# Two-layer encoder on one core: a gate half computed earlier, a turn moved to TensorE, and a bias table read backwards through GpSimd's queue

## The chip, the core and the metric

The kernel runs on one core of one Trainium2 chip. A core has five engines with a queue of instructions each: TensorE (PE in the profile, with the loads of its weights as PEld), VectorE (DVE), ScalarE (ACT), GpSimd (POOL) and SyncE (SP), which here only starts transfers. Each takes its own queue in order, and they wait for each other by semaphores. The metric is device microseconds of one execution of the whole program. Three runs of the kernel before took 883.23, 883.34 and 884.79 us, a median of 883.34 us.

## The reference

The input is one sequence of 256 tokens with 1024 channels in float32. Two layers follow each other, then a last normalisation. In short:

```
h = x
for layer in range(2):
    xn = rmsnorm(h) * norm1
    u, q, k, v, g_pool, g_attn = split(xn @ w_in)      # 1024 x 7680
    pool = centred means of u over 2/4/8/16 tokens, minus u, times w_pool
    attn = three groups of four heads, windows of 129 keys at stride 1, 4, 16,
           logits + bias(relative position), softmax over all three groups
    merged = sigmoid(g_pool) * (pool @ w_a) + sigmoid(g_attn) * (attn @ w_b)
    h += merged @ w_o
    xn = rmsnorm(h) * norm2
    a, g = split(xn @ w_up)                            # 1024 x 5632
    h += (gelu(conv3(a)) * g) @ w_down
out = rmsnorm(h) * norm_f
```

The bias depends only on the distance between query and key. The tokens are held by even and odd position, so that a tile of 128 queries against 128 keys needs 255 distances for each of five kinds of pair.

## The kernel before, in words

Every float32 product is made of three products of rounded parts: a value is split into a high part (`wh`, `xh`, written by ScalarE as a copy, line 179) and a low part (`wl`, the rest, by VectorE as a subtraction, line 180), and TensorE adds high times high, high times low and low times high. So each weight piece of 128 x 1024 numbers costs one ScalarE cast and one VectorE subtraction before TensorE may use it.

The class `Weights` orders this. All weights of the program stand in one list, in the order of their use. SyncE loads them, 1 MB at a time, into three buffers (`raw`); each load serves two pieces; a piece goes into one of five pairs of buffers (`wh`, `wl`). `get` hands out a piece and has the next three (`LOOK`) split ahead. A `raw` buffer is free when both of its pieces are split, a `wh`/`wl` pair when TensorE is through with it. Some pieces at the beginning of a sub-layer get buffers of their own (`slots`). The order on each engine is set by a scheduler that places the instructions by their estimated readiness; the order on one engine is then fixed.

A layer goes through these stages, each with TensorE as the engine that all feed:

- values, pooling inputs, queries and keys, by `proj` (16 products a piece, lines 490 and 492);
- the stage called gates here, by `by_rows` (line 594): products of 128 x 512, twelve for each piece. One of its halves is 512 of the 1024 output channels. The kernel before does the pool gate (`C_GP`, 8 pieces), then `w_a` (8 pieces), then for each half the attention gate (`C_GA`, 4 pieces) and `w_b` (2 pieces). `po2` holds the pooled part, `at2` the attention's, `pa` what the pool branch gives, `th` the merged rows of a half.
- in between, `step` puts in the attention of the first heads at numbered visits, one visit after each piece: scores, turning of the probabilities, their parts, and the weighting. `VISITS` has the numbers.
- `w_o`, by `residual_mm` (line 521): eight pieces, each against the merged rows turned into channels (`m2`, high part `mh`, low part `ml`). Pieces 0 to 3 are added into four accumulators as they come; pieces 4 to 7 are held, and the accumulators are finished one after another, so that the normalisation of the first tokens starts early.
- the MLP, in the same manner, its first four pieces from `w_up` in slots.

The merged rows have tokens on partitions, and `w_o` needs channels there. The kernel before turns the first half by one transposition in blocks of 32 on VectorE (line 1063) and 16 transfers between partitions (`cross`, line 609, `way<-way` in the profile) which SyncE starts during the second half; `merged_parts` splits what comes back (lines 1047 and 1048). The second half is turned on VectorE alone, by 32 transpositions of single blocks (`blocks`, line 617, tile `turned`), and split by lines 1077 and 1078.

The bias table is built once, in `build_bias`: TensorE sums the buckets, VectorE copies the rows to `fsb` (line 384), three transfers put them in one row in memory (`fd`, 20 KB), one transfer copies this row 128 times, each time one further (`sk`, 2.56 MB, line 393), and five transfers read from `sk` the table `bt` (line 398), with 128 keys for each of 128 queries. All nine are started by SyncE, between the weight loads. `bias_of` hands the part of `bt` to the addition at line 917.

Of the kernel before, what the change touches and what calls it, by code (L numbers as in the profile page):

```python
# [55 lines left out]
def _bias_table():  # L56

    t = np.zeros((33, NT, 256), np.float32)
    delta = np.arange(255) - 127
    for n, (e, dil) in enumerate(  # L60
        ((2 * delta, 1), (2 * delta + 1, 1), (2 * delta - 1, 1), (2 * delta, 4), (2 * delta, 16))
    ):
        valid = (e % dil == 0) & (np.abs(e) <= 64 * dil)
        b = _buckets(e)
        j = np.nonzero(valid)[0]
        t[b[j], n, j] = 1.0
        t[32, n, np.nonzero(~valid)[0]] = NEG
        t[32, n, 255] = NEG
    return t.reshape(33, NT * 256)


def _edge_table():
# [134 lines left out]
def encoder(ctx, tc, x, w_in, w_pool, pool_scale, w_a, w_b, w_o, norm1, norm2, w_up, conv_w,  # L207
# [166 lines left out]
    def build_bias(rr, ohr):  # L374

        fsb = big.tile([96, NT * 256], F32, tag="q1", name="fsb")
        for c0, groups in ((0, (0, 0)), (512, (0, 1)), (1024, (2,))):
            width = 256 * len(groups)
            ps = acc.tile([P, 512], F32, tag="acc", name="f_ps")
            nc.tensor.matmul(ps[:, :width], rr, ohr[:, c0 : c0 + width], start=True, stop=True)  # L380
            for j, g in enumerate(groups):
                cc = slice(j * 256, (j + 1) * 256)
                rows = slice(32 * g, 32 * g + HPG)
                nc.vector.tensor_copy(fsb[rows, c0 + j * 256 : c0 + (j + 1) * 256], ps[rows, cc])
            yield

        n = HPG * NT * 256
        fd = dram.tile([1, n], F32, name="fd")
        fv = fd[0].rearrange("(h e) -> h e", h=HPG)
        for g, cc in enumerate((slice(0, 768), slice(768, 1024), slice(1024, 1280))):  # L390
            nc.sync.dma_start(out=fv[:, cc], in_=fsb[32 * g : 32 * g + HPG, cc])
        sk = dram.tile([P, n + 1], F32, name="sk")
        nc.sync.dma_start(out=sk[:, 0:n], in_=fd[0].partition_broadcast(P))
        for blk, kind in enumerate((2, 0, 1, 3, 4)):
            src = bass.AP(
                sk.tensor, sk.offset + kind * 256 + 127, [[n, P], [NT * 256, HPG], [1, P]]
            )
            nc.sync.dma_start(out=bt[:, :, blk * P : (blk + 1) * P], in_=src)
# [386 lines left out]
    for l in range(DEPTH):  # L785
# [115 lines left out]
        def scores(hh):  # L901
            probs[hh] = sm.tile([P, 2, 512], F32, tag="s", name="probs")
            for t in range(2):
# [6 lines left out]
                for g in (1, 2):  # L910
# [4 lines left out]
                    )  # L915
                s = probs[hh][:, t]
                nc.vector.tensor_add(
                    out=s.rearrange("p (a b) -> p a b", a=2), in0=ps.rearrange("p (a b) -> p a b", a=2),
                    in1=bias_of(t, hh),
                )  # L920
                nm = sm.tile([P, 1], F32, tag="nm", name="nm")
                nc.vector.tensor_reduce(out=nm, in_=s, axis=AX.X, op=ALU.max, negate=True)
# [98 lines left out]
        for n, cc in enumerate(HALVES):  # L1021
# [5 lines left out]
        for cc in HALVES:  # L1027
            ps = by_rows(po2, 4, step)
# [5 lines left out]
        assert not any(visits) and not crossing  # L1034
        g2 = gain(norm2[l])


        m2 = big.tile([P, 2, KD, 2, P], F32R, tag="m2", name="m2")
        mh, ml = m2[:, 0], m2[:, 1]
        way = big.tile([P, 2, 4, 2, 4, 32], F32, tag="k1", name="way")  # L1040
        def merged_parts():
            yield from cross(way[:, 1], way[:, 0])
            yield
            for t in range(2):
                m = way[:, 1, :, t].rearrange("p i c r -> p c i r")
                hi, lo = (a[:, 0:4, t].rearrange("p c (i r) -> p c i r", i=4) for a in (mh, ml))
                nc.scalar.copy(out=hi, in_=m)  # L1047
                nc.vector.tensor_sub(out=lo, in0=m, in1=hi.bitcast(F32))

        for n, cc in enumerate(HALVES):  # L1050
            ps = by_rows(x2, 4, n and (lambda: next(first, None)))
            th = big.tile([P, 2, 512], F32, tag=("q0", "k0")[n], name="th")
            for t in range(2):
                nc.scalar.activation(th[:, t], ps[t], AF.Tanh, scale=0.5)
            ps = by_rows(at2, 2, n and (lambda: next(first, None)))
            for t in range(2):
                p = th[:, t]
                nc.vector.scalar_tensor_tensor(
                    out=p, in0=p, scalar=1.0, in1=ps[t], op0=ALU.add, op1=ALU.mult
                )  # L1060
                nc.vector.tensor_add(out=p, in0=p, in1=pa[:, t, cc])
            if n == 0:
                nc.vector.transpose(
                    out=way[:, 0].rearrange("p j t c r -> p (t c) j r"),
                    in_=th.rearrange("p t (c j r) -> p (t c) j r", c=4, j=4),
                )
                first = merged_parts()
            else:
                assert next(first, None) is None
                turned = big.tile([P, 4, 2, P], F32, tag="v0", name="turned")  # L1070
                for k in range(0, 4, 2):
                    run(blocks(
                        turned[:, k : k + 2].rearrange("p c t q -> p t c q"),
                        th[:, :, k * P : (k + 2) * P].rearrange("p t (c k) -> p t c k", c=2),
                    ))
                    hi, lo = (a[:, 4 + k : 6 + k] for a in (mh, ml))
                    nc.scalar.copy(out=hi, in_=turned[:, k : k + 2])
                    nc.vector.tensor_sub(out=lo, in0=turned[:, k : k + 2], in1=hi.bitcast(F32))

        x2 = two_parts("x", "x2")  # L1080
        norm = Norm(to_channels(x2, acc, g2))
# [137 lines left out]
```

## Time and profile before

| | |
|---|---|
| median of three runs | 883.34 us (883.23 to 884.79) |
| the profiled execution | 885.41 us, its span 883.6 us |
| TensorE busy | 864.5 us, 98% of the span |
| VectorE busy | 689.0 us, 78% |
| ScalarE busy | 496.1 us, 56% |
| transfers | 169.86 MB, 192 GB/s over the span |
| mean granted clock of TensorE | 0.994 |

A line of the timeline gives the start, the duration, the engine, the line of the kernel, the operation, the tile written and the tiles read, the shape and the count; in brackets stands the idle time of the engine before it, with what ended it. A start minus the start before it is the time that an instruction held its engine; the duration of a matmul reaches over the start of the next one, because they are pipelined. In the table of windows, PEclk is the clock that TensorE was granted, as a share of its full clock. SPq is SyncE's queue, where the bar is the time in which it issues a transfer, not the transfer.

### The profile page before, as it was taken

How to read it: one execution, taken by the hardware profiler on the slowest of the kernel's cores; microseconds unless marked ns; L12 is line 12 of the kernel's file. 1: busy time of each engine (PE TensorE's matmuls, PEld its weight loads, DVE VectorE, ACT ScalarE, POOL GpSimd, SP SyncE). 2: the span in 40 equal slices, each digit the busy share in tenths (PEclk: the TensorE clock that was granted, in tenths of full speed). 3: DMA queues.
4: the chain of work that ended last, by engine and by line, in shares of the span. 5: the costliest groups of instructions: out<-in, count | busy, mean ns of one | idle time of the engine just before them, and what ended most of it. 6: DMA issues, size and time to landing. Idle time of an engine off the chain costs nothing.

```text
span 883.6 us, 12221 instructions
## 1 busy us (share of the span) xinstructions
PE 864.5 (98%) x4538; PEld 740.3 (84%) x4538; DVE 689.0 (78%) x1148; ACT 496.1 (56%) x817; POOL 17.3 (2%) x45
## 2 busy tenths in 40 slices
PE   9999999999899999999999999999997999999997
PEld 7887988888778888888888899888885888888886
DVE  7996895756788998779755968785569799887884
ACT  7754654534436766667545555464443567666662
POOL 2000000000010000000000000000000100000000
PEclk9999999999999999999999999999999999999999
DMA  9677836565454475665726555547644556565541
GB/s 337 207 234 233 276 119 226 169 236 193 165 190 159 176 238 169 217 207 169 263 96 212 170 193 189 179 155 238 215 145 162 173 189 237 191 198 183 191 144 49
DMA packets 118408, 169.86 MB, mean 192 GB/s; under 512 B 4790, under 2 KB 84358, under 8 KB 118220
## 3 DMA queue, kind: packets, MB, share of 16 engines
q1 hardware_dynamic: 118332, 169.07, 57.0%
q8 instruction: 36, 0.59, 0.3%
q14 instruction: 24, 0.20, 0.1%
q10 hardware_dynamic: 16, 0.00, 0.0%
HBM read 162.74 MB, written 3.69 MB: 188 GB/s over the span
## 4 chain that ended last, share of the span: by engine, by line
PE 87%; DVE 5%; DMA 4%; SPq 2%; ACT 1%; issue 1%; POOL 0%; POOLq 0%; ACTq 0%
PE proj_ps L490 28%; PE rows_ps L587 15%; PE proj_ps L492 14%; PE v_ps L587 6%; PE res_ps L518 5%; PE res_ps L517 5%; PE res_ps L519 5%; PE v_ps L777 2%; DVE turned L617 2%; DMA sk<-fd 2%; PE v_ps L690 1%; DMA raw<-in_w_up_dram 1%; DVE wl L180 1%; SPq L609 1%; PE o_ps L968 1%; PE s_ps L911 1%
## 5 line engine op out<-in xcount | busy, mean ns | idle before, releaser
L180 DVE TENSOR_TENSOR wl<-raw,wh 128x1024 fp32r<-128x1024 f32 x274 | 332.6, 1221 | 114.1 <-ACT wh L179 111.7
L179 ACT CAST wh<-raw 128x1024 fp32r<-128x1024 f32 x274 | 285.4, 1048 | 172.7 <-PE proj_ps L490 63.2
L490 PE MATMUL proj_ps<-x,wh 128*128 128x512 f32 x1152 | 289.9, 394 | 1.8 <-ACT wh L179 1.8
L490 PEld LDWEIGHTS proj_ps<-x,wh 128*128 128x128 f32 x1152 | 209.0, 189 | 40.2 <-ACT wh L179 2.0
L492 PEld LDWEIGHTS proj_ps<-x,wl 128*128 128x128 f32 x1152 | 157.6, 191 | 11.4
L492 PE MATMUL proj_ps<-x,wl 128*128 128x256 f32 x1152 | 161.0, 282 | 0.0
L587 PE MATMUL rows_ps<-wh,x 128*128 128x512 f32 x256 | 80.9, 391 | 0.0
L517 PE MATMUL res_ps<-wh,actq 128*128 128x512 f32 (+1 forms) x184 | 70.2, 381 | 0.0
L518 PE MATMUL res_ps<-wl,actq 128*128 128x512 f32 (+1 forms) x184 | 70.1, 381 | 0.0
L519 PE MATMUL res_ps<-wh,actk 128*128 128x512 f32 (+1 forms) x184 | 69.9, 380 | 0.0
L587 PEld LDWEIGHTS rows_ps<-wh,x 128*128 128x128 f32 x256 | 48.1, 188 | 9.8
L587 PE MATMUL rows_ps<-wl,x 128*128 128x512 f32 x128 | 49.8, 389 | 0.0
L587 PE MATMUL rows_ps<-wh,po 128*128 128x512 f32 x128 | 40.6, 391 | 0.0
L519 PEld LDWEIGHTS res_ps<-wh,actk 128*128 128x128 f32 x184 | 34.6, 188 | 6.6
L517 PEld LDWEIGHTS res_ps<-wh,actq 128*128 128x128 f32 x184 | 34.7, 188 | 6.2
L518 PEld LDWEIGHTS res_ps<-wl,actq 128*128 128x128 f32 x184 | 34.7, 188 | 6.0
L1132 ACT ACTIVATE y<-a,prm 128x256 f32<-128x256 f32 x36 | 21.6, 600 | 22.2 <-DVE a L513 22.2
L517 PE MATMUL res_ps<-wh,m 128*128 128x512 f32 (+1 forms) x72 | 27.0, 380 | 5.2 <-ACT m L1047 5.2
L518 PE MATMUL res_ps<-wl,m 128*128 128x512 f32 (+1 forms) x72 | 27.6, 383 | 3.7 <-DVE wl L180 3.7
L1149 ACT ACTIVATE y<-y 128x256 f32<-128x256 f32 x44 | 18.3, 416 | 21.3 <-DVE y L1146 21.2
L587 PEld LDWEIGHTS rows_ps<-wh,po 128*128 128x128 f32 x128 | 24.0, 188 | 5.0
L587 PEld LDWEIGHTS rows_ps<-wl,x 128*128 128x128 f32 x128 | 24.1, 188 | 4.9
(206 smaller groups left out, 1150.4 us busy)
## 6 DMA issues: line engine op xcount, KB each, us to landing
raw<-in_w_in_dram SPq DMA_DIRECT2D x58, 1024.0 KB
raw<-in_w_up_dram SPq DMA_DIRECT2D x44, 1024.0 KB
raw<-in_w_down_dram SPq DMA_DIRECT2D x22, 1024.0 KB
raw<-in_w_a_dram SPq DMA_DIRECT2D x8, 1024.0 KB
raw<-in_w_o_dram SPq DMA_DIRECT2D x8, 1024.0 KB
pt<-rows SPq DMA_DIRECT2D x64, 64.0 KB
raw<-in_w_b_dram SPq DMA_DIRECT2D x4, 1024.0 KB
sk<-fd SPq DMA_DIRECT2D x1, 2560.0 KB
```

Source lines behind the costliest of these rows:

```text
L179: lambda: nc.scalar.copy(out=h, in_=src),
L180: lambda: nc.vector.tensor_sub(out=l, in0=src, in1=h.bitcast(F32)),
L490: nc.tensor.matmul(ps, wh(k), x2[:, k], start=(k == 0), stop=False)
L492: nc.tensor.matmul(ps[:, 1], wl(k), x2[:, k, 0], start=False, stop=(k == nk - 1))
L517: nc.tensor.matmul(ps, ah, wh, start=first, stop=False)
L518: nc.tensor.matmul(ps, ah, wl, start=False, stop=False)
L519: nc.tensor.matmul(ps, al, wh, start=False, stop=last)
L587: nc.tensor.matmul(ps, x2[:, 2 * n + j, part, t, :], w[:, j, :], start=(n + m == 0), stop=(n == of - 1 and m == 5),)
L617: nc.vector.transpose(out=out[b, :, :, a], in_=in_[a, :, :, b])
L777: nc.tensor.matmul(ps[t], a[:, k, t, :], w[:, j, :], start=(k + m == 0), stop=(k == KD - 1 and m == 2),)
L1132: nc.scalar.activation(y, a, AF.Identity, bias=b, scale=w1)
L1149: nc.scalar.activation(y2, y2, AF.Tanh, scale=c)
```

## The change

Three things are changed, and nothing in what is computed.

First, the order of the gates stage: pool gate (both halves), then for each half `w_a`, attention gate and `w_b`. The merged rows of the first half are so complete before the second half of `w_a` begins, and its crossing and splitting go on during the second half's ten pieces, where they had six. The last visits of two heads move one or two pieces later.

Second, the second half of the merged rows is no longer turned by VectorE: after the first and the second piece of `w_o`, TensorE turns four blocks of 128 x 128 each by products with the identity (`mt_ps`), and the parts are split from there.

Third, the bias table: the table of buckets is stored backwards, `sk` and its transfer are gone, `bt` is read from the row `fd` directly, with each partition beginning one number further; all eight transfers are started by GpSimd; and the addition reads `bt` with a step of -1.

```
-VISITS = ((0, 1, 12, 13), (2, 3, 14, 15), (9, 10, 21, 22), (10, 11, 22, 23))
+VISITS = ((0, 1, 12, 14), (2, 3, 15, 16), (9, 10, 22, 23), (10, 11, 23, 24))
...
-    return t.reshape(33, NT * 256)
+    return np.roll(t[:, :, ::-1], -1, axis=2).reshape(33, NT * 256)
...
-        for w, c0 in ((w_in[l], C_GP), (w_a[l], 0)):
-            for half in HALVES:
-                for j in range(2):
-                    W.use(rows(w, j * 512, 4, c0 + half.start, 512))
         for half in HALVES:
-            for j in range(2):
-                W.use(rows(w_in[l], j * 512, 4, C_GA + half.start, 512))
-            W.use(rows(w_b[l], 0, 4, half.start, 512))
+            half_of(w_in[l], C_GP, half, 2)
+        for half in HALVES:
+            half_of(w_a[l], 0, half, 2)
+            half_of(w_in[l], C_GA, half, 2)
+            half_of(w_b[l], 0, half, 1)
...
-            nc.sync.dma_start(out=fv[:, cc], in_=fsb[32 * g : 32 * g + HPG, cc])
-        sk = dram.tile([P, n + 1], F32, name="sk")
-        nc.sync.dma_start(out=sk[:, 0:n], in_=fd[0].partition_broadcast(P))
+            nc.gpsimd.dma_start(out=fv[:, cc], in_=fsb[32 * g : 32 * g + HPG, cc])
         for blk, kind in enumerate((2, 0, 1, 3, 4)):
-            src = bass.AP(
-                sk.tensor, sk.offset + kind * 256 + 127, [[n, P], [NT * 256, HPG], [1, P]]
-            )
-            nc.sync.dma_start(out=bt[:, :, blk * P : (blk + 1) * P], in_=src)
+            src = bass.AP(fd.tensor, fd.offset + kind * 256, [[1, P], [NT * 256, HPG], [1, P]])
+            nc.gpsimd.dma_start(out=bt[:, :, blk * P : (blk + 1) * P], in_=src)
...
-        if t == 0:
-            return bt[:, hh, P:].rearrange("p (a b) -> p a b", a=2)
-        b = bt[:, hh, 0:256]
+        b = bt[:, hh, P - 1 :] if t else bt[:, hh, 2 * P - 1 :]
         (pstep, pn), _ = b.ap
-        return bass.AP(b.tensor, b.offset, [[pstep, pn], [3 * P, 2], [1, 256]])
+        return bass.AP(b.tensor, b.offset, [[pstep, pn], [(2, 3)[t] * P, 2], [P, 2], [-1, P]])
...
+        def merged(n, cc, visit):
+
+            ps = by_rows(po2, 4, visit)
...
+            ps = by_rows(x2, 4, visit)
             th = big.tile([P, 2, 512], F32, tag=("q0", "k0")[n], name="th")
             for t in range(2):
                 nc.scalar.activation(th[:, t], ps[t], AF.Tanh, scale=0.5)
-            ps = by_rows(at2, 2, n and (lambda: next(first, None)))
+            ps = by_rows(at2, 2, n and visit)
...
+        th = merged(0, HALVES[0], step)
...
+        def first_half():
+            yield from cross(way[:, 1], way[:, 0])
+            for _ in range(2):
+                yield
+            for t in range(2):
+                yield
+                keep_merged(0, t, way[:, 1, :, t].rearrange("p i c r -> p c i r"))
+
+        first = first_half()
+        th = merged(1, HALVES[1], lambda: next(first, None))
...
-                turned = big.tile([P, 4, 2, P], F32, tag="v0", name="turned")
-                for k in range(0, 4, 2):
-                    run(blocks(
...
-        run(residual_mm(lambda k: (mh[:, k], ml[:, k]), KD, norm.add, fill=begin_mlp))
+        out_mm = residual_mm(lambda k: (m2[0][:, k], m2[1][:, k]), KD, norm.add, fill=begin_mlp)
+        for t in range(2):
+            next(out_mm)
+            pt = mmp.tile([P, 4, P], F32, tag="mm", name="mt_ps")
+            for k in range(4):
+                nc.tensor.transpose(pt[:, k, :], th[:, t, k * P : (k + 1) * P], ident)
+            keep_merged(4, t, pt)
+        run(out_mm)
```

`keep_merged` is the pair of lines that splits four channel blocks: a cast on ScalarE, a subtraction on VectorE.

More of the change, by code (lines that the diff above doesn't have):

```diff
@@ L260, in encoder, with half_of @@
             W.use(q + k)
-        for w, c0 in ((w_in[l], C_GP), (w_a[l], 0)):
-            for half in HALVES:
-                for j in range(2):
-                    W.use(rows(w, j * 512, 4, c0 + half.start, 512))
+        def half_of(w, c0, half, n):
+            for j in range(n):
+                W.use(rows(w, j * 512, 4, c0 + half.start, 512))
         for half in HALVES:
-            for j in range(2):
-                W.use(rows(w_in[l], j * 512, 4, C_GA + half.start, 512))
-            W.use(rows(w_b[l], 0, 4, half.start, 512))
+            half_of(w_in[l], C_GP, half, 2)
[3 more added lines that the diff above has]
+            half_of(w_b[l], 0, half, 1)
         for c in range(4):
@@ L917, in scores @@
                 nc.vector.tensor_add(
-                    out=s.rearrange("p (a b) -> p a b", a=2), in0=ps.rearrange("p (a b) -> p a b", a=2),
-                    in1=bias_of(t, hh),
+                    out=s.rearrange("p (a b c) -> p a b c", a=2, b=2),
+                    in0=ps.rearrange("p (a b c) -> p a b c", a=2, b=2), in1=bias_of(t, hh),
                 )
@@ L1026, in encoder @@
                 nc.scalar.activation(pa[:, t, cc], ps[t], AF.Tanh, scale=0.5)
-        for cc in HALVES:
-            ps = by_rows(po2, 4, step)
+        way = big.tile([P, 2, 4, 2, 4, 32], F32, tag="k1", name="way")
+        def merged(n, cc, visit):
+            ps = by_rows(po2, 4, visit)
             for t in range(2):
@@ L1033, in encoder @@
                 )
[L1034 to L1051, printed above, removed]
+            if n:
+                two = big.tile([P, 2, KD, 2, P], F32R, tag="m2", name="m2")
+                m2.extend((two[:, 0], two[:, 1]))
+            ps = by_rows(x2, 4, visit)
             th = big.tile([P, 2, 512], F32, tag=("q0", "k0")[n], name="th")
@@ L1061, in encoder, with keep_merged @@
                 nc.vector.tensor_add(out=p, in0=p, in1=pa[:, t, cc])
[L1062 to L1069, printed above, removed]
-                turned = big.tile([P, 4, 2, P], F32, tag="v0", name="turned")
-                for k in range(0, 4, 2):
-                    run(blocks(
[L1073 to L1078, printed above, removed]
+            return th
+        def keep_merged(c0, t, m):
+            hi, lo = (a[:, c0 : c0 + 4, t] for a in m2)
+            if len(m.ap) == 4:
+                hi, lo = (a.rearrange("p c (i r) -> p c i r", i=4) for a in (hi, lo))
+            nc.scalar.copy(out=hi, in_=m)
+            nc.vector.tensor_sub(out=lo, in0=m, in1=hi.bitcast(F32))
+        m2 = []
+        th = merged(0, HALVES[0], step)
+        assert not any(visits) and not crossing
+        g2 = gain(norm2[l])
+        nc.vector.transpose(
+            out=way[:, 0].rearrange("p j t c r -> p (t c) j r"),
+            in_=th.rearrange("p t (c j r) -> p (t c) j r", c=4, j=4),
+        )
+        def first_half():
[7 more added lines that the diff above has]
+        th = merged(1, HALVES[1], lambda: next(first, None))
         x2 = two_parts("x", "x2")
```

3 lines of the change are left out of this document (1 added, 2 removed).

## The prediction

> **What bounds the kernel now.** I read first the busy times and the chain of waits that ended last, then TensorE's own waits, then the timelines around each of them.
>
> ```profile
> PE 864.5 (98%) x4538; PEld 740.3 (84%) x4538; DVE 689.0 (78%) x1148; ACT 496.1 (56%) x817; POOL 17.3 (2%) x45
> ...
> PE res_ps L517 <- ACT m L1047: 5.2, 2, 2.6
> PE res_ps L518 <- DVE wl L180: 3.7, 6, 1.9
> PE proj_ps L490 <- ACT wh L179: 1.8, 1, 1.8
> ```
>
> TensorE is the bound, and what can be won is only the time in which it stands or runs slowly. It waits at three places: for the turned merged rows (`m`, 5.2 us in two waits), for low parts of `w_o` (six times, 3.7 us), once in a projection (1.8 us). The change touches all three. A wait costs more than its idle time, so I take each place from start to start.
>
> The place in the projections, on TensorE and then in the chain of waits:
>
> ```profile
> 78.98 2.00 PE L490 MATMUL proj_ps<-x,wh 128*128 128x512 f32 x8
> 80.83 1.11 PE L492 MATMUL proj_ps<-x,wl 128*128 128x256 f32 x8
> 83.69 3.48 PE L490 MATMUL proj_ps<-x,wh 128*128 128x512 f32 x8 [1.75 <-ACT wh L179]
> 88.15 0.28 PE L482 MATMUL pool_ps<-plh,wh 128*128 128x256 f32 x1
> ...
> 57.17 13.76 DMA sk<-fd
> 70.94 0.62 SPq L398
> 75.58 6.94 DMA raw<-in_w_in_dram
> ...
> 70.00:90.00 20.00, 18.25 (x101) 15.94 (x100) 11.84 (x17) 8.95 (x15) 0.00 (x0) 0.91 0.76 244
> 231.00:262.00 31.00, 26.99 (x122) 21.47 (x123) 28.73 (x60) 13.72 (x23) 2.32 (x5) 0.94 0.50 178
> 664.00:694.00 30.00, 24.95 (x119) 19.68 (x120) 27.63 (x57) 13.31 (x22) 2.14 (x5) 1.00 0.49 175
> ```
>
> Eight long products take 1.85 us (78.98 to 80.83) and eight short ones 0.95, since a piece repeats every 2.79. From 80.83 to 88.15 are 7.32 us for 0.95 + 1.85 + 0.95 = 3.75: 3.6 us are lost. Of these 1.9 are the gap (81.78 to 83.69), the other 1.7 the slow products after it, with a granted clock of 0.91 in the window. The chain names the cause: the transfer `sk<-fd` runs 13.76 us, SyncE stands until it is done to issue the five `bt` reads, and the weight load behind them goes out at 75.58 only.
>
> The place at `w_o`, layer 0 and then layer 1:
>
> ```profile
> 230.57 0.39 PE L587 MATMUL rows_ps<-wh,at 128*128 128x512 f32 x1
> ...
> 239.41 0.39 PE L517 MATMUL res_ps<-wh,m 128*128 128x512 f32 x1
> 246.21 0.39 PE L517 MATMUL res_ps<-wh,m 128*128 128x512 f32 x1
> 256.32 0.28 PE L517 MATMUL res_ps<-wh,m 128*128 128x256 f32 x1
> 257.75 0.60 PE L458 MATMUL xt_ps<-ident,xn 128*128 128x128 f32 x4
> 258.11 0.36 PE L517 MATMUL res_ps<-wh,m 128*128 128x256 f32 x1
> 258.31 0.28 PE L518 MATMUL res_ps<-wl,m 128*128 128x256 f32 x1
> ...
> 663.06 0.39 PE L587 MATMUL rows_ps<-wh,at 128*128 128x512 f32 x1
> ...
> 690.18 0.65 PE L458 MATMUL xt_ps<-ident,xn 128*128 128x128 f32 x4
> ```
>
> Between 239.41 and 246.21 stand 30 products: 0.227 us each. From the last gate product to the first `xt_ps` are 85 of these (one, 48 of pieces 0 to 3, 36 of the first three finished accumulators), 19.3 us, and twelve short ones from 256.32 to 257.75, 1.4 us: 20.7 us of work. It took 27.18 us in layer 0 and 27.12 in layer 1: 6.5 and 6.4 us lost. Layer 0 ran slowly after its gap of 2.6 us (0.94 in the window), layer 1 did not (1.00), and both lose the same: what sets the end here is not TensorE's clock but a chain on VectorE.
>
> ```profile
> 230.51 1.28 DVE L1058 SCALAR_TENSOR_TENSOR th<-th,rows_ps 128x512 f32<-128x512 f32 x2
> 231.71 1.29 DVE L1061 TENSOR_TENSOR th<-th,pa 128x512 f32<-128x512 f32 x2
> 233.58 1.29 DVE L1048 TENSOR_TENSOR m<-way,m 128x512 fp32r<-128x512 f32 x2 [0.59 <-ACT m L1047]
> 234.79 6.32 DVE L617 STREAM_TRANSPOSE turned<-th 32x128 f32<-32x128 f32 x20
> 241.83 3.79 DVE L617 STREAM_TRANSPOSE turned<-th 32x128 f32<-32x128 f32 x12
> 245.65 2.36 DVE L180 TENSOR_TENSOR wl<-raw,wh 128x1024 fp32r<-128x1024 f32 x2
> ```
>
> The 32 block transpositions hold VectorE for 10.1 us, and the next low parts of `w_o` stand behind them until 245.65.
>
> **The change, part by part.** *Bias table.* SyncE loses nine issues and the wait. The load of 75.58 then waits only for its buffer, whose second piece is split here:
>
> ```profile
> 67.88 1.22 DVE L180 TENSOR_TENSOR wl<-raw,wh 128x1024 fp32r<-128x1024 f32 x1
> ...
> 52.67 0.42 DVE L384 COPY fsb<-f_ps 4x256 f32<-4x256 f32 x1
> ...
> L917 DVE TENSOR_TENSOR probs<-s_ps,bt x16: 669/680/692, 112.5 to 589.7; 128x512 f32<-128x512 f32 x16
> L928 DVE TENSOR_SCALAR probs<-probs,rz x16: 445/478/487, 115.5 to 594.6; 128x512 f32<-128x512 f32 x16
> ```
>
> It goes out at 69.1, lands 6.94 later at 76.0, and TensorE needs it at 81.8 with a cast before: some 4 us to spare. So the 3.6 us go. GpSimd issues eight transfers, three and then five, from 53.1 on. No row shows its queue. Lower bound: as on SyncE, where a `bt` issue takes 0.62 us. Upper bound: each of the two steps takes as long as `sk<-fd`, which moves ten times the bytes of one `bt` read: 53.1 + 27.5 = 80.6. The first addition that reads `bt` is at 112.5, so both ends cost nothing; behind them GpSimd has nothing until the normalisation beyond 250 us. Reading `bt` backwards: 16 additions of 0.68 us; a gain is not to be had, a second pass over the table would add 0.68 each, 5.4 us of VectorE a layer. I take 0, since addition and reduction of one pass both take 0.68 here.
>
> By the Trainium skill ("SBUF — State Buffer", section "SBUF: two separate sides") a transfer that GpSimd starts is stalled while VectorE runs an operation that takes the port pair the two share. In this trace the first operation on 512 numbers that is faster than one pass, a sign of that mode, is `L928`, at 115.5, behind the first use of `bt`; so by that rule, too, the sum would stand.
>
> *Gates one half early.* The products are the same in number. In the trace the first half's way from TensorE to channels ends with the subtraction at 233.58 + 1.29 = 234.9. SyncE's sixteen copies fill most of it:
>
> ```profile
> 219.03 7.49 SPq L609 DMA_DIRECT2D way<-way  x12
> 226.62 0.53 SPq L119 DMA_DIRECT2D raw<-in_w_o_dram  x1
> 227.19 2.40 SPq L609 DMA_DIRECT2D way<-way  x4
> ...
> 229.01 3.60 DMA way<-way
> ...
> 253.22 1.06 ACT L179 CAST at<-raw 128x1024 fp32r<-128x1024 f32 x1 [6.94 <-DMA raw<-in_w_up_dram]
> ```
>
> The first half's last product was 72 products (16.3 us) before 230.57, so the way takes 20.6 us; with the second half of `w_a` in between TensorE needs 120 products, 27.2 us. It ends 6.6 us before `w_o` needs it: the waits for `m` go. The third `w_o` load, issued behind twelve copies at 226.62, also comes earlier against TensorE.
>
> *Second half turned on TensorE.* VectorE loses 10.1 us a layer; what it is late with next is listed under the rivals. TensorE gains eight transpositions a layer. Four of the same shape hold it 0.36 us (257.75 to 258.11), and the product after them 0.20 instead of 0.12: 0.44 for four, 1.8 us for both layers, all on the path. `th` of the first tokens is ready at 231.71 + 0.64 = 232.4; piece 0 of `w_o` would end at 230.8 + 12 x 0.227 = 233.5: TensorE need not wait, with 1.1 us to spare. The splits from `mt_ps` replace those from `turned` one for one.
>
> *Later visits.* The last head's scores come 12 products (2.7 us) later, and its weighting stands 4 products (0.9 us) earlier in TensorE's order.
>
> ```profile
> 173.11 2.44 SPq L609 DMA_DIRECT2D pt<-rows  x4
> ...
> 182.33 0.71 ACT L954 CAST pth<-pt 128x256 fp32r<-128x256 f32 x2
> ```
>
> The last copy is issued at about 175.0; `way`'s last landed 3.6 us after its issue began (229.01, above), so the probabilities are there at 178.6, 3.7 us before the cast: 3.6 of these are used up. I put 0.3 us a layer for it, between 0 and 1.5.
>
> *Sum* against the profiled 885.41 us (span 883.6): -3.6 - 6.5 - 6.4 + 1.8 + 0.6 = -14.1, that is 871.3. This execution is 2.1 us above the median of 883.34, and slow clock after a gap need not come in each (layer 1 shows none); without the 1.7 us of it in the projections the change brings 12.4 from the median: 870.9. I forecast **871 us**.
>
> By the Trainium skill ("TensorE: Matmul & The Clock Gate", "Part 1: The HAM clock gate (the "warmup" mystery)") the clock halves after an idle window of some 3.4 us; here it fell after a gap of 1.75 us and stayed up in layer 1 after one of about 2.6, so the trace doesn't follow the figure. If the gap is not the cause, the slow stretch stays somewhere, and 883.34 - 12.4 holds rather than the first sum.
>
> **The rivals.** *A part of the stall at `w_o` comes back.* In the changed order of VectorE and ScalarE the splits of `w_up`'s first load stand ahead of those of `w_o`'s last two pieces. That load can go out only when piece 3 is split, near the end of the gates stage, and lands 5 to 7 us later; in the trace ScalarE stood 6.94 us for such a load. With 5 us there remain about 2 us before TensorE needs piece 7; with 7 or more, or with `th` late by over 1.1 us, TensorE stands 1 to 3 us in each layer, 873 to 877. A backwards read at two passes, where VectorE's slack doesn't cover it, ends in the same range.
>
> *The stall only changes its name.* If `w_o` is bound by loads throughout, its 12.9 us stay, the transpositions cost 1.8, and the projections bring 1.9: 883.2, no change. For it speaks the wait of 6.94; against it that the loads before it were in time, and were issued late because of the copies.
>
> *Slower: GpSimd's queue is slow.* VectorE takes its queue in order, so a late `bt` holds everything behind the addition at 112.5, and TensorE has three pieces of 2.79 us split ahead. Slower than before it would be if `bt` came after 112.5 + 8.4 + 12.4 = 133.3, which is 10 us for each of the eight transfers if they go one by one. At 13.76 each, the length of `sk<-fd`, `bt` would come at 163.2, and the time would be 871 + 163.2 - 120.9 = 913. Against it: the five reads don't depend on each other, and the same bytes from SyncE's queue took no such time.
>
> **How the numbers follow.** All three parts as computed: 0.64, 869 to 873. Part of the stall back: 0.22, 873 to 877. Name changed: 0.05. Slow queue: 0.07. Better than computed, because VectorE's relief also shortens the start of the MLP: 0.02. Range 867 to 878, the likeliest case and the second. A difference under 0.2% (1.8 us) can't be told from none: faster 0.88, same 0.05, slower 0.07.
>
> **What would show it.** Right: no wait of TensorE for `wh` near 80 us; no `sk`; the stage from the last gate product to `xt_ps` at 21.6 to 22.5 us in both layers; no `turned`, eight `mt_ps` a layer without a wait before them; additions with `bt` at 0.68. Wrong: `res_ps` waiting for `wl` or `wh` of `w_o`'s last pieces, `o_ps` waiting for `ptl`, `mt_ps` for `th`, or VectorE standing at the first `probs`.

## The result and the profile after

The kernel after takes 869.91 us (median of 4 runs, 869.54 to 871.30) against 883.65 us (4 runs, 883.23 to 884.79): the ratio is 0.9845, 95% interval 0.9828 to 0.9862, or 13.7 us less. 871 us was predicted, and 869.91 lies inside the range of 867 to 878. The profiled execution took 870.25 us with a span of 868.5 us, 15.1 less than the span of the one before.

The busy times on the page of the kernel after, and all waits of its TensorE:

```profile
PE 860.7 (99%) x4554; PEld 740.9 (85%) x4554; DVE 670.5 (77%) x1084; ACT 496.8 (57%) x817; POOL 21.1 (2%) x53
...
PE gain_ps L334 <- DVE ones L320: 1.0, 1, 1.0
PE v_ps L685 <- ACT xuh L641: 0.2, 1, 0.2
```

The three waits named in the prediction (`m`, `wl`, `wh`) are gone. TensorE has 16 instructions more, the transpositions, in 3.8 us less of busy time: fewer of its products ran at a slow clock (the mean granted clock is 0.998, it was 0.994).

TensorE in the projections, SyncE's queue beside them, and the additions and transfers of `bt`:

```profile
78.73 1.11 PE L487 MATMUL proj_ps<-x,wl 128*128 128x256 f32 x8
79.69 2.00 PE L485 MATMUL proj_ps<-x,wh 128*128 128x512 f32 x8
81.53 1.11 PE L487 MATMUL proj_ps<-x,wl 128*128 128x256 f32 x8
82.48 2.00 PE L485 MATMUL proj_ps<-x,wh 128*128 128x512 f32 x8
...
70.73 5.21 SPq L119 DMA_DIRECT2D raw<-in_w_in_dram  x2
...
L912 DVE TENSOR_TENSOR probs<-s_ps,bt x16: 653/681/692, 109.6 to 583.6; 128x512 f32<-128x512 f32 x16
L395 POOL DMA_DIRECT2D bt<-fd x5: 749/749/807, 56.1 to 59.1; - x5
...
DMA to landing us min/median/max: 4.5/7.1/7.4
```

The pieces follow each other every 2.79 us without a gap. The load that used to go out at 75.58 goes out at 70.73. The last `bt` read is issued at 59.1 and none took over 7.4 us to land, so the table is there by 66.5, 43 us ahead of the first addition at 109.6. The additions that read it backwards take 681 ns; forwards they took 680.

TensorE around `w_o`, layer 0 (last gate product, first product of `w_o`, the turned second half, first `xt_ps`), then layer 1 (last gate product, `xt_ps`):

```profile
227.75 0.39 PE L582 MATMUL rows_ps<-wh,at 128*128 128x512 f32 x1
227.98 0.39 PE L512 MATMUL res_ps<-wh,m 128*128 128x512 f32 x1
...
230.71 0.60 PE L1093 MATMUL mt_ps<-ident,th 128*128 128x128 f32 x4
...
233.92 0.60 PE L1093 MATMUL mt_ps<-ident,th 128*128 128x128 f32 x4
...
249.45 0.60 PE L453 MATMUL xt_ps<-ident,xn 128*128 128x128 f32 x4
...
654.21 0.39 PE L582 MATMUL rows_ps<-wh,at 128*128 128x512 f32 x1
...
675.91 0.60 PE L453 MATMUL xt_ps<-ident,xn 128*128 128x128 f32 x4
```

The stage takes 21.70 us in both layers, against 27.18 and 27.12.

From such starts the span can be cut at the same places in every kernel: the two small products `prm_ps` that start 0.12 us ahead of the first `proj_ps` and count as its beginning, the first `pool_ps`, the last gate product, the first `xt_ps`, and the first `proj_ps` of the MLP, the last three in each layer. Lengths in us:

| stretch | before | after | difference |
|---|---|---|---|
| to the first `proj_ps` | 41.60 | 42.30 | +0.70 |
| projections to `pool_ps` | 46.55 | 42.97 | -3.58 |
| to the last gate product | 142.42 | 142.48 | +0.06 |
| `w_o`, layer 0 | 27.18 | 21.70 | -5.48 |
| start of the MLP, layer 0 | 14.81 | 14.21 | -0.60 |
| to the last gate product, layer 1 | 390.50 | 390.55 | +0.05 |
| `w_o`, layer 1 | 27.12 | 21.70 | -5.42 |
| start of the MLP, layer 1 | 15.20 | 14.21 | -0.99 |
| rest | 178.22 | 178.38 | +0.16 |
| span | 883.6 | 868.5 | -15.1 |

Two rows were not in the prediction. The first 42 us differ by 0.70 although the change leaves them alone; two further profiles with the new table have 41.61 and 41.62 there, so this is a difference between executions. The start of the MLP, which follows `w_o`, became 1.6 us shorter over both layers.

### The profile page after: what moved, and what is told of

It is laid out like the page before. It is cut to its first block, busy times and chain, and to the rows that moved or that the text cites. A ratio compares the mean times of both kernels' runs of the same rounds, so it can differ in the third digit from the quotient of the medians.

```text
span 868.5 us, 12204 instructions
## 1 busy us (share of the span) xinstructions
PE 860.7 (99%) x4554; PEld 740.9 (85%) x4554; DVE 670.5 (77%) x1084; ACT 496.8 (57%) x817; POOL 21.1 (2%) x53
## 3 DMA queue, kind: packets, MB, share of 16 engines
HBM read 160.12 MB, written 1.07 MB: 186 GB/s over the span
## 4 chain that ended last, share of the span: by engine, by line
PE 99%; ACT 0%; POOLq 0%; DVE 0%; issue 0%; POOL 0%; ACTq 0%
PE proj_ps L485 30%; PE rows_ps L582 18%; PE proj_ps L487 16%; PE res_ps L512 6%; PE res_ps L513 6%; PE v_ps L582 6%; PE res_ps L514 6%; PE v_ps L772 3%; PE v_ps L685 1%; PE o_ps L963 1%; PE s_ps L906 1%; PE o_ps L959 1%; PE s_ps L901 1%; PE xt_ps L453 1%; PE pool_ps L479 0%; PE pool_ps L478 0%
## 5 line engine op out<-in xcount | busy, mean ns | idle before, releaser
L1134 ACT ACTIVATE y<-a,prm 128x256 f32<-128x256 f32 x36 | 21.6, 600 | 21.9 <-DVE a L508 21.9
L419 ACT ACTIVATE junk<-h 128x512 f32<-128x512 f32 (+1 forms) x20 | 10.9, 547 | 27.1 <-DVE h L417 27.1
```

The source lines that it names most:

```text
L419: nc.scalar.activation(junk[:, 0 : cc.stop - cc.start], h[:, t, cc], AF.Square, scale=D**-0.5, accum_out=ss[:, n : n + 1],)
L1134: nc.scalar.activation(y, a, AF.Identity, bias=b, scale=w1)
```

## The experiments

**The bias part alone, undone and done.** The old table, read forwards, the copy `sk` and SyncE's queue in the kernel after (the main lines of the edit, here and below):

```
+        sk = dram.tile([P, n + 1], F32, name="sk")
+        nc.sync.dma_start(out=sk[:, 0:n], in_=fd[0].partition_broadcast(P))
...
+            nc.sync.dma_start(out=bt[:, :, blk * P : (blk + 1) * P], in_=src)
```

> The kernel after, with the bias part alone undone: the old table, the expanded copy sk, all nine transfers on SyncE's queue, the table read forwards. Theory (SyncE's wait for sk holds the next weight load, TensorE stands for 1.9 us and its clock then falls for another 1.7 us): 869.9 + 3.6 = 873.5 us, a gap of about 1.75 us before a proj_ps near 84 us and a granted clock near 0.91 behind it. If the fall of the clock has nothing to do with the gap, 871.8 us and no slow products. Rival (the bias part brings nothing, the load is late in any case): 869.9 us.

Measured: 870.39 us (5 runs, 869.91 to 871.22), 0.5 us above the kernel after. Its TensorE and SyncE at the place of the gap:

```profile
80.82 1.11 PE L494 MATMUL proj_ps<-x,wl 128*128 128x256 f32 x8
81.95 2.12 PE L492 MATMUL proj_ps<-x,wh 128*128 128x512 f32 x8
...
74.53 11.28 SPq L119 DMA_DIRECT2D raw<-in_w_in_dram  x3
```

The load goes out 1.05 us earlier than in the first profile of the kernel before, and the next piece starts only 0.2 us late (80.82 + 0.95 would be 81.77). The stretch takes 43.24 us (41.61 to 84.85). And the reverse, the new table in the kernel before:

```
-        sk = dram.tile([P, n + 1], F32, name="sk")
...
+            src = bass.AP(fd.tensor, fd.offset + kind * 256, [[1, P], [NT * 256, HPG], [1, P]])
+            nc.gpsimd.dma_start(out=bt[:, :, blk * P : (blk + 1) * P], in_=src)
```

> The kernel before with the bias part alone: the new table, eight transfers on GpSimd's queue, the table read backwards. Theory: 883.65 - 3.6 = 880.1 us, no gap in the projections, both waits at w_o as before (stage of 27.1 us). With the gap alone and no effect on the clock 881.8 us. Rival (a wait removed early comes back at w_o, where VectorE sets the end): 883.6 us.

Measured: 883.01 us (12 runs, 881.97 to 884.08) beside 883.74 (17 runs, 881.96 to 888.25), ratio 0.9988, interval 0.9977 to 0.9999. The projections take 42.98 us without a gap, but its profile shows 28.46 and 27.39 us for the stage of `w_o`, where 27.1 was expected: of what this execution won in the projections, some was lost there, as the rival had it. So the table is worth at most some 0.7 us of the median, not 3.6. In the kernel after, it can't be told from nothing: with the old table it takes 870.39 us, and with the new table on SyncE's queue and no gap (further down) 870.31.

**The kernel before, profiled once more**, without any edit, to see whether the gap belongs to the kernel.

> The kernel before, unchanged, profiled once more. Theory (the late load of 75.58 us lands at the very moment at which TensorE wants it, so the gap of 1.75 us belongs to one execution and not to the kernel): a gap between 0 and 1.8 us before a proj_ps near 82 us, its size following the moment at which the load is issued, and slow products behind it only if it is long. Rival (the gap is the same each time, and the kernel after wins its 3.6 us in another way than by the table): 1.7 to 1.8 us again.

It took 883.28 us, with a span of 881.5. Its TensorE and SyncE around the place, and its windows:

```profile
80.79 1.11 PE L492 MATMUL proj_ps<-x,wl 128*128 128x256 f32 x8
82.71 2.12 PE L490 MATMUL proj_ps<-x,wh 128*128 128x512 f32 x8 [0.81 <-ACT wh L179]
...
70.49 4.13 SPq L398 DMA_DIRECT2D bt<-sk  x5
74.74 1.63 SPq L119 DMA_DIRECT2D raw<-in_w_in_dram  x2
...
70.00:90.00 20.00, 19.19 (x117) 16.96 (x116) 13.03 (x21) 9.27 (x15) 0.00 (x0) 1.00 0.79 255
231.00:262.00 31.00, 27.92 (x133) 22.44 (x134) 28.25 (x59) 12.56 (x23) 3.17 (x7) 1.00 0.51 180
664.00:694.00 30.00, 28.38 (x128) 22.29 (x129) 27.06 (x56) 12.37 (x22) 2.90 (x7) 0.95 0.47 164
```

The gap is 0.81 us here, with the full clock behind it (1.00 for the window 70 to 90, where the first profile had 0.91), and the projections take 44.04 us. Together with the first profile and the kernel with the old table there are three profiles of this code: the load went out at 75.58, 74.74 and 74.53 us, and the stretch took 46.55, 44.04 and 43.24 us against 42.97 without `sk`, a loss of 3.58, 1.07 and 0.27. One microsecond in the issue of a load decides it: `sk` lets the load land right at the moment at which TensorE wants it. The first profile, on which the prediction was summed, has the largest loss of the three.

**The copy or SyncE's wait for it?** Two kernels were to separate the two. The new table with its eight transfers on SyncE's queue:

```
-            nc.gpsimd.dma_start(out=bt[:, :, blk * P : (blk + 1) * P], in_=src)
+            nc.sync.dma_start(out=bt[:, :, blk * P : (blk + 1) * P], in_=src)
```

> The kernel after with its eight transfers of the table issued by SyncE instead of GpSimd; no sk, the table read backwards. Theory (only the wait for the 13 us of sk holds the weight load; the five bt issues of some 0.7 us each fit before its buffer is free): the load goes out at 70 to 72 us, no gap, 42.97 us from the first projection to the first pool_ps as in the kernel after, 869.9 us. Rival (any issue on SyncE there delays the load past its margin): a gap of over 0.2 us and a later load, 870.5 us and more.

870.31 us (4 runs, 870.00 to 870.51), the load at 70.03 us, 42.98 us for the stretch: for the small table the queue doesn't matter. And the old table with `sk`, with all nine transfers on GpSimd's queue:

```
+        sk = dram.tile([P, n + 1], F32, name="sk")
+        nc.gpsimd.dma_start(out=sk[:, 0:n], in_=fd[0].partition_broadcast(P))
```

> The kernel after with the old table and the copy sk, but all nine transfers on GpSimd's queue. Theory (SyncE's wait was what held the load, not the 2.6 MB that sk writes): the load goes out at 70 to 71 us, no gap, 42.97 us from the first projection to the first pool_ps; bt lands at about 80 us, 30 us before its use: 869.9 us. Rival (the traffic of sk delays the load itself): it lands after 80.6 us and TensorE stands again, 870.5 us and more.

873.02 us (4 runs, 871.94 to 874.96), 3.1 us slower than the kernel after, though SyncE no longer waits for the copy. Its transfers issued between 56 and 58 us, the load behind them on SyncE, and TensorE where it stands; then the same transfer in the kernel after:

```profile
sk<-fd POOLq DMA_DIRECT2D x1, 2560.0 KB, 11.8
raw<-in_w_in_dram SPq DMA_DIRECT2D x1, 1024.0 KB, 14.1
...
74.66 15.45 SPq L119 DMA_DIRECT2D raw<-in_w_in_dram  x5
...
88.64 1.65 PE L492 MATMUL proj_ps<-x,wh 128*128 128x512 f32 x3 [1.62 <-DVE q L1017]
```

```profile
raw<-in_w_in_dram SPq DMA_DIRECT2D x1, 1024.0 KB, 9.7
```

On its own queue `sk` starts ahead of a weight load (55.81 against 56.87) instead of behind it, and that load takes 14.1 us to land instead of 9.7. Its splits come late, so its buffer is free late, and the next load goes out at 74.66 instead of the expected 70 to 71. VectorE catches up with the late splits in order, and TensorE waits for `q` behind them: 1.6 us, and slow products after it (0.88 in the window 78 to 92). The stretch to `pool_ps` still takes 42.96 us; the loss lies behind it. So this run's theory fails, and its rival holds: with the copy there, freeing SyncE wins nothing. Two things changed at once, though, the queue and the order: in the first profile of the kernel before, where `sk` starts 0.58 us behind the weight load, ScalarE splits that load from 64.31 on, at most 7.7 us after its issue at 56.59. And SyncE's standing is still what that profile shows for the load of 75.58. Without the copy either queue will do; with it a load came late on either queue, not the same one.

**The order without TensorE's turning.** The second half turned on VectorE again, in the new order:

```
-            pt = mmp.tile([P, 4, P], F32, tag="mm", name="mt_ps")
-            for k in range(4):
-                nc.tensor.transpose(pt[:, k, :], th[:, t, k * P : (k + 1) * P], ident)
-            keep_merged(4, t, pt)
+        turned = big.tile([P, 4, 2, P], F32, tag="v0", name="turned")
+        for k in range(0, 4, 2):
+            run(blocks(
+                turned[:, k : k + 2].rearrange("p c t q -> p t c q"),
+                th[:, :, k * P : (k + 2) * P].rearrange("p t (c k) -> p t c k", c=2),
+            ))
...
```

> The kernel after, with the second half of the merged rows turned on VectorE again (32 block transposes a layer) and the new order of the gates kept. Theory (the 10.1 us of transposes are a chain that sets the end of w_o): th is ready at about 230.9 us, the transposes and the subtraction of the last two chunks end about 13 us later at 244 us, where TensorE wants piece 7 at about 241, and the splits of w_o stand behind them: 3 to 6 us lost a layer, less 0.9 us for TensorE's transpositions, and the MLP's start loses its 0.8 to 1.0 us again: 876 to 882 us, with waits of res_ps for m or wl. Rival (once the first half is done early, pieces 0 to 3 with their 10.9 us of products hide the transposes): 868 to 870 us.

Measured: 880.59 us (4 runs, 879.52 to 880.96). VectorE's timeline and TensorE's waits:

```profile
230.63 6.33 DVE L612 STREAM_TRANSPOSE turned<-th 32x128 f32<-32x128 f32 x20
236.99 0.69 DVE L1097 TENSOR_TENSOR m<-turned,m 128x512 fp32r<-128x512 f32 x1
237.72 3.78 DVE L612 STREAM_TRANSPOSE turned<-th 32x128 f32<-32x128 f32 x12
241.53 1.22 DVE L180 TENSOR_TENSOR wl<-raw,wh 128x1024 fp32r<-128x1024 f32 x1
...
PE res_ps L513 <- DVE wl L180: 6.9, 2, 3.5
```

The wait for `m` of the first half is gone, so the new order does its part. What waits is a low part of `w_o`, 3.5 us a layer, split at 241.53 behind the transposes. This is the chain that the prediction named. Behind the two waits TensorE runs slowly (0.89 in the window 231 to 262, 0.94 in 664 to 694).

**TensorE's turning without the order.** The kernel before with the new table, and `mt_ps` in place of `turned`:

```
-                turned = big.tile([P, 4, 2, P], F32, tag="v0", name="turned")
-                for k in range(0, 4, 2):
-                    run(blocks(
...
+        for t in range(2):
+            next(out_mm)
+            pt = mmp.tile([P, 4, P], F32, tag="mm", name="mt_ps")
+            for k in range(4):
+                nc.tensor.transpose(pt[:, k, :], th[:, t, k * P : (k + 1) * P], ident)
...
```

> The kernel after with the old order of the gates and the old visits, the second half turned by TensorE as in the kernel after. Theory (the first half's way of 20.6 us ends 3.4 to 4.1 us after the last gate product): one wait of res_ps for m of 3 to 4 us at the first product of w_o in each layer, none for wl: 877 to 878.5 us. Rival 1 (the transposes alone made the stall and the order brings nothing): 870 us. Rival 2 (the order alone makes it, TensorE's turning brings nothing): about 880 us.

Measured: 876.23 us (4 runs, 875.01 to 877.68). Its TensorE's waits, and its windows:

```profile
PE mt_ps L1082 <- DVE th L1054: 3.1, 2, 1.6
...
PE res_ps L510 <- ACT m L1040: 1.0, 2, 0.6
...
231.00:262.00 31.00, 31.00 (x154) 26.02 (x153) 19.17 (x28) 13.52 (x24) 2.16 (x7) 0.94 0.53 183
```

The stage takes 25.77 and 25.89 us, 4.1 and 4.2 more than in the kernel after, and the time lies 0.8 us under the expected 877 to 878.5. The two waits come to 2.1 us a layer, where one of 3 to 4 was expected, and the name is another: the planner (the scheduler that places the instructions) put the first transpositions ahead of `w_o`'s first product, and so TensorE stands for `th` first and for `m` only 0.6 us more; slow products follow (0.94).

All four combinations have the new table: neither part 883.01, the order alone 880.59 (-2.4), the turning alone 876.23 (-6.8), both 869.91 (-13.1). Together they bring 3.9 us more than the sum of each. The first half's way and the transposes are two chains that end close to each other; with one removed, TensorE still stands for the other, and runs slowly behind that wait. An estimate of these slow products is the busy time of TensorE times what its clock lacks, in the windows 226 to 272 and 652 to 706: 42.53 x 0.07 + 50.25 x 0.03 = 4.5 us with the order alone, 43.97 x 0.04 + 51.86 x 0.03 = 3.3 us with the turning alone, nothing in the kernel after. They go only with the last wait, and are more than the 3.9.

**How much room VectorE has.** More passes over the second half of `th` before its last addition, one at first:

```
+                for _ in range(1 * n):
+                    nc.vector.tensor_max(out=p, in0=p, in1=p)
```

> The kernel after with one more pass of VectorE over each of the two second halves of th (th = max(th, th), 0.65 us each). Theory (th of the first tokens is ready 1.2 us before TensorE turns it, and the last low part of w_o 2.2 us before its use): th comes 0.65 to 1.3 us later, inside the margin: 869.9 us, at most 0.3 more. Rival (a chain on VectorE sets the end of w_o still): 1.3 us a layer, 872.5 us.

869.45 us (4 runs, 869.39 to 870.91): nothing lost, as expected. With `range(4 * n)`:

> The kernel after with four more passes of VectorE over each second half of th (2.6 us each, 5.2 a layer). Theory: th of the first tokens comes 2.6 to 5.2 us later, 1.4 to 4.0 beyond its margin, and what waits is mt_ps; the last low part of w_o comes 5.2 us later, 3 beyond its margin. TensorE stands 2 to 4 us a layer, and where its clock falls after the gap another 1 to 1.5: 873 to 880 us. Rival (TensorE can go on with other products and VectorE has the time to spare): 870 us.

870.35 us (4 runs, 869.88 to 870.47). The theory failed, and the rival was right. TensorE and VectorE of that kernel:

```profile
234.26 1.14 PE L1095 MATMUL mt_ps<-ident,th 128*128 128x128 f32 x8
...
228.58 4.90 DVE L1046 TENSOR_TENSOR th<-th 128x512 f32<-128x512 f32 x8
233.40 1.28 DVE L1047 TENSOR_TENSOR th<-th,pa 128x512 f32<-128x512 f32 x2
```

`th` is ready 4.5 us later than in the kernel after (233.40 against 228.89 for the start of its additions), and all eight transpositions stand at 234.26 without a wait. The planner had put more products of `w_o` ahead of them, so the 1.1 us between `th` and the end of piece 0 were never a limit. With `range(8 * n)`, which costs VectorE about as much as the 32 block transposes:

> The kernel after with eight more passes of VectorE over each second half of th: 16 passes of 0.61 us a layer, 9.8 us, as much of VectorE as the 32 block transposes of the kernel before. Four passes cost nothing, since all eight transpositions were put behind later products of w_o (at 234.26 us) and the last split of w_o still came at 240.4. Theory (what counts is VectorE's time between th and the last split of w_o, whatever it is spent on): 4.9 us more than with four passes, so th is ready at about 239.6 us, the splits of m end near 242 to 243 and those of w_o near 245, against about 239.7 and 242 at which TensorE wants them: 3 to 5 us a layer, and up to 1 more at the start of the MLP: 876 to 881 us. Rival (the block transposes cost by something of their own, not by VectorE's time): 870 to 872 us.

```profile
228.33 9.72 DVE L1046 TENSOR_TENSOR th<-th 128x512 f32<-128x512 f32 x16
237.96 1.29 DVE L1047 TENSOR_TENSOR th<-th,pa 128x512 f32<-128x512 f32 x2
239.16 1.22 DVE L180 TENSOR_TENSOR wl<-raw,wh 128x1024 fp32r<-128x1024 f32 x1
240.30 1.28 DVE L1055 TENSOR_TENSOR m<-mt_ps,m 128x512 fp32r<-128x512 f32 x2
241.50 3.49 DVE L180 TENSOR_TENSOR wl<-raw,wh 128x1024 fp32r<-128x1024 f32 x3
```

875.85 us (4 runs, 875.61 to 877.12), 5.9 us lost, just under the expected 876 to 881. VectorE has 4.9 us a layer to spare, and not 9.7. What TensorE stands for is not a low part of `w_o`, as the theory had it:

```profile
PE xt_ps L453 <- DVE xn L444: 1.6, 2, 0.8
```

All 48 products of pieces 0 to 3 stand ahead of the transpositions here (238.70), and the lateness of VectorE comes out mostly at the normalised rows `xn` (1.6 us in both layers together, 0.5 at `th`). The 10.1 us of transposes cost 10.7 in the experiment above, 9.7 us of plain passes 5.9. The windows name most of the difference of 4.8: there the wait of 3.5 us had slow products behind it, by the estimate above 4.5 us; here the clock stays at 1.00. The comparison is rough, since the kernel with the transposes is spared TensorE's eight `mt_ps` a layer. That the block transposes cost something of their own, beside VectorE's time, isn't shown.

**A late table.** Twenty copies of the small table, one after the other, on GpSimd's queue ahead of the reads:

```
+        fe = dram.tile([1, HPG * NT * 256], F32, name="fe")
+        for _ in range(10):
+            nc.gpsimd.dma_start(out=fe[0], in_=fd[0])
+            nc.gpsimd.dma_start(out=fd[0], in_=fe[0])
```

> The kernel after with twenty copies of the small table, each waiting for the one before, on GpSimd's queue ahead of the five bt reads; at an estimated 4 us each bt lands some 80 us later, at 147 us instead of 66.5. Theory (VectorE takes its queue in order and stands at the first addition, at 109.6 us here; TensorE has 8.4 us of split pieces ahead): the loss is the landing of bt less 118 us, about 29 us, so 899 us, with VectorE idle at probs and TensorE idle behind it for a weight piece. Rival 1 (VectorE works on past the addition): under 5 us lost. Rival 2 (a late table costs more than its lateness, since the two layers share it or the clock falls): over 35 us.

892.46 us (one run). The waits of TensorE and VectorE, and two windows:

```profile
PE proj_ps L489 <- ACT wh L179: 15.5, 1, 15.5
PE o_ps L963 <- ACT pth L953: 1.3, 1, 1.3
...
DVE probs L916 <- DMA bt<-fd: 23.2, 1, 23.2
...
120.00:130.00 10.00, 1.62 (x11) 1.30 (x10) 0.00 (x0) 0.00 (x0) 4.77 (x7) 0.76 0.40 94
130.00:150.00 20.00, 12.71 (x56) 10.79 (x57) 17.35 (x32) 9.72 (x19) 0.00 (x0) 0.69 0.20 46
```

The twenty copies took 3.5 us each (55.51 to 124.55) rather than 4, and VectorE got the table at 132.6. By the formula of the expectation that costs 132.6 - 118 = 14.6 us, and TensorE did stand 15.5. But the span grew by 22.2 us. TensorE's clock was at 0.50 in the window 135 to 140, 0.76 in 140 to 145 and 1.00 in 145 to 150, so the piece behind the gap took 5.6 us (137.09 to 142.72, with a wait of 0.2) instead of 2.79; then later visits came late (`o_ps`, 2.0 us in two waits), with 0.83 in the window 160 to 170. So the mechanism is the one told, VectorE in order and nothing else to do, and the price is half again as large. By the Trainium skill ("TensorE: Matmul & The Clock Gate", "Part 1: The HAM clock gate (the "warmup" mystery)") the clock halves after an idle window of about 3.4 us; this gap of 15.5 us, with 0.50 behind it, agrees with it. The gaps of 1.75 us in the first profile and of 1.6 us at `mt_ps` don't: slow products followed both.

## Why the prediction was right, point by point

**The total** was right, 871 against 869.91, with errors that partly cancel: the table was put too high, the start of the MLP was left out, and the later visits were given a price that they don't have. That they cancel is luck; the stage of `w_o`, most of the sum, is not.

**The bias term** (-3.6, or -1.9 by the gap alone) failed in size. It is exact for the profiled execution (-3.58), but that one lay 1.8 us above the median, and its stretch was 2.5 us longer than in the second profile of the kernel before, which took 883.28 us. In the medians the term is at most some -0.7. The prediction saw that the slow clock need not come each time and went to 12.4 us from the median; it did not doubt the gap itself, which was 1.75, 0.81 and nearly none in three profiles. Its cause was half right: the load was late through `sk`, but the copy on the other queue was worse (873.02), and the small table on SyncE took 870.31 us, no gap in its projections. The load was predicted for 69.1 and went out at 70.73, with time to spare.

**The stage of `w_o`** (-6.5 and -6.4, and 0.44 for each four transpositions) was right: 27.2 - 6.5 + 0.9 is 21.6, and it takes 21.70. That a chain on VectorE set its end is borne out by the order alone (880.59) and by 16 plain passes (875.85).

**The first half's way** was right. Its last subtraction of the first half was to be 6.6 us ahead of `w_o`; by the first row below it ends at 222.2, 5.7 us ahead of 227.98, and TensorE has no wait for `m`. The load of `w_up` was to be the danger, with 2 us to spare at piece 7. ScalarE waited 0.48 us for it, and the last low part of `w_o` was split from 238.42 to 239.65 (second row), while TensorE comes to it at about 241.8, 2 us later: 48 products of pieces 0 to 3 and nine of the first finished accumulator from 227.98 on, at 0.227 us each, and 0.9 for the transpositions between.

```profile
220.95 1.29 DVE L1053 TENSOR_TENSOR m<-way,m 128x512 fp32r<-128x512 f32 x2
...
238.42 1.23 DVE L180 TENSOR_TENSOR wl<-raw,wh 128x1024 fp32r<-128x1024 f32 x1 [0.32 <-ACT wh L179]
...
232.92 1.05 ACT L179 CAST v<-raw 128x1024 fp32r<-128x1024 f32 x1 [0.48 <-DMA raw<-in_w_up_dram]
```

**The 1.1 us of `th`** were measured well (the first half of the additions ends near 229.5, the transpositions start at 230.71), but the conclusion was wrong: a later `th` doesn't stop TensorE, since its order isn't bound to the text of the program. The price of 1 to 3 us a layer for a late `th` should have begun only several us later.

**Later visits** (+0.3 a layer) cost nothing: 142.42 us became 142.48, 390.50 became 390.55, and `o_ps` has no wait. By the numbers in `VISITS` each moved visit comes one piece later, not one or two.

**The start of the MLP** was the step left out, given 2 in 100 as a rival. It brought 0.60 and 0.99 us. With TensorE's turning alone it is 14.16 us in both layers; with the transposes on VectorE it is 14.50 and 15.28 (new table alone) or 14.34 and 14.99 (order alone). So it goes with the transposes. How is not shown: the wait of `v_ps` for `x` on VectorE, 0.8 us in the first profile, is gone with the turning alone, but with the order alone too.

**The rivals.** Part of the stall coming back and the stall changing its name did not happen; the waits of the page show neither. The slow queue did not happen in the kernel after, where `bt` has 43 us to spare, but its break-even was put too late: 133.3 us was to be no gain and no loss, and at 132.6 the kernel took 892.46 us, some 22 us more than the kernel after and 9 more than before.

**Sum from the median.** The order and the turning, with the start of the MLP, bring 13.1 us (883.01 to 869.91), the table at most 0.7; the whole is 13.7.

## What to carry to other kernels

A gap in one profiled execution that lies above the median may be that execution's own: a load that lands within a microsecond of its use makes a different gap each time, so compare a second profile before its full length goes into a sum. Where two chains end at the same consumer, removing one shows less than its share (here 2.4 or 6.8 us of 13.1); count what ends next before pricing either. A margin read between two instructions on an engine holds only for that order, and a planner that sees a later producer may choose another.

## What the runs showed that was not expected

A weight load of 1 MB took 14.1 us to land when a copy of 2.6 MB had been started 1.06 us ahead of it from another queue, 9.7 us beside the five small reads, and at most 7.7 us with the copy 0.58 us behind it on its own queue. Moving that copy off the queue that it blocked made the kernel 2.6 us slower than leaving it there (873.02 against 870.39).

TensorE's clock fell after some short gaps and not after others: 0.91 behind the gap of 1.75 us and 1.00 behind that of 0.81 in two profiles of the same kernel, and at `w_o`, with the same work, 0.94 and 1.00 for the two layers in the first and 1.00 and 0.95 in the second. Behind the gaps of 1.75 and 1.6 us it fell to a half, and for about 3.5 us: in windows of 1 us it is 0.53 or 0.50 from 84 to 87 and 1.00 from 88 in the first profile, 0.52 or 0.50 from 231 to 234 and 1.00 from 235 with the turning alone. By estimate half of that time is lost, some 1.7 us beside the gap, as the prediction had it for the first profile.

Reading the table backwards costs no time: 681 ns for an addition of 128x512 against 680.
